# Group norms of a hybrid decoder layer: sums over partitions by two products of ones with the split squares, the sums issued a tick earlier, a small state tile in another pool, and the first masking of a state renewal placed later

## The chip, the cores and the metric

The kernel runs on one core of a Trainium2 chip. The time is that of one execution in device microseconds; the number for a kernel is the median of several executions. The times shown for the kernel before are 1761.23 us in the median of three, from 1761.22 to 1761.29.

## The reference, cut to what matters

One layer of a hybrid decoder runs over 320 tokens: 256 of a prompt and 64 (8 sequences of 8) that continue older sequences. A combined projection feeds a gated MLP and a state space mixer; their outputs go through one output projection, and a feed forward part with a short convolution follows. All of it is in 32-bit floats. The two places that the change touches are the norm inside the mixer, over four groups of 512 channels, and the recurrent states of the 8 continued sequences, which are renewed from their new tokens:

```python
y = y.reshape(bsz, L, SSM_WIDTH) * jax.nn.silu(z.astype(f32))
yg = y.reshape(bsz, L, SSM_GROUPS, SSM_WIDTH // SSM_GROUPS)
yg = yg * lax.rsqrt(jnp.mean(yg * yg, axis=-1, keepdims=True) + EPS)
y = yg.reshape(bsz, L, SSM_WIDTH) * norm_w.astype(f32)
...
up, new_conv = causal_depthwise_conv(up, conv_state, conv_w, conv_b)   # conv_ffn
```

## The kernel before, in words

**Layout and products.** Channels lie on the 128 partitions and the 320 tokens (`NT`) along the free axis. Every weight matrix comes in slabs of 512 KB (`slab`, DMA issued on SP at L126). ScalarE rounds a slab to the reduced format that TensorE streams in one pass (`whi`, L130), VectorE makes the rest (`wlo`, L132), each of `wraw`, `whi` and `wlo` in three buffers. Each 128x128 block then takes three matmuls of 320 columns (L143 to L145): high by high, high by low, low by high. A slab is 8 blocks, that is 24 matmuls.

**Order.** The program is written in the order of the products. Everything else hangs in a list of tasks (`bg`), Python generators of which `tick()` advances the first by one `yield` after a slab (after some slabs twice or three times, `rate`). A planner then sets each engine's own order from priorities and estimated times; `first()` raises a priority, and `tc.issue_after(x)` keeps an instruction behind `x`. Each engine runs its instructions strictly in its own order.

**Group norm** (`heads_out`, `norm`). For each of the four groups, `z_evac` builds `ssq` (128x320): per partition and token the sum of four squares. `norm` then needs the sum over the 128 partitions. `token_sums` (L284) takes three matmuls in full 32-bit floats, with 128 tokens of `ssq` as the stationary operand and one column of ones, which leave the sums as columns `tsum` with tokens on partitions. `rsqrt_of` (L250 to L256) takes the inverse root of these 128x3 numbers by eleven small VectorE instructions, a first guess and three Newton steps. `spread` (L292) brings the three columns back by three transposes, as a 128x320 tile in PSUM with the same value in every partition. VectorE multiplies the four tiles of `y` by it (L960; the tile is called `xs` in the profile), and `split` makes `ohi` and `olo` of them for the output projection (L373, L374; for the last group the buffers of `h_hi` and `h_lo` are used). `later` is the pair of ticks that `norm` lets pass before its sums and before `spread`.

**Convolution states of the feed forward part** (`ffn_up`). `fst` is a small tile (two buffers) of earlier rows; SP loads it at L1073. It lies in the pool `fp`, which takes the memory of pools that are closed before it.

**Renewal of states** (`renewals`). For each of four groups `tokens` loads decayed rows into `raw` by 16 small DMAs (L1180, tile `xb`). ScalarE copies them to `part` (L1191, `xb_parts`), VectorE masks the copy in place (L1194), and after some ticks TensorE takes four products of it (L1211, `up_ps`), which VectorE adds to the states `st` (L1213). GpSimd has multiplied the states by their decays before (L1199).

Of the kernel before, what the change touches and what calls it, by code (L numbers as in the profile page):

```python
# [9 lines left out]
F32 = mybir.dt.float32  # L10
F32R = mybir.dt.float32r
I32 = mybir.dt.int32
AF = mybir.ActivationFunctionType
ALU = mybir.AluOpType
# [3 lines left out]
P = 128  # L18
NP = 256
NB, TS = 8, 8  # L20
NS = NB * TS
NT = NP + NS
# [12 lines left out]
def hybrid_step(  # L35
# [14 lines left out]
    cp = ctx.enter_context(tc.tile_pool(name="cp", bufs=1))  # L50
# [6 lines left out]
    def misc(name):  # L57
        return ms.tile([P, 512], F32, tag="ms", name=name)
# [6 lines left out]
    with tc.high_priority(offset=300000):  # L65
        dve.memset(ones, 1.0)

        ps = misc("early")
        for _ in range(EARLY):
            pe.matmul(ps[:, :P], ones, ones, start=True, stop=True)  # L70
    upper = cp.tile([P, P], F32, name="upper")
    later = cp.tile([P, P], F32, name="later")
    bd2 = cp.tile([P, P], F32, name="bd2")
# [3 lines left out]
    bd = bd2[:NS, :NS]  # L77

    def masks():
        make_upper_triangular(nc, upper, 1.0, diag=True)  # L80
        make_lower_triangular(nc, later, 1.0, diag=False)
        pool.memset(bd2, 0.0)
        for op, fill, base in ((ALU.is_gt, 1.0, 1 - TS), (ALU.is_ge, 0.0, 0)):
            pool.affine_select(out=bd2, in_=bd2, pattern=[[-TS, P // TS], [0, TS]], compare_op=op, fill=fill, base=base,
                               channel_multiplier=1)

        d4 = ident.rearrange("p (i r t) -> p i r t", r=4, t=TS)
        dve.tensor_reduce(out=low[:, 0:1], in_=d4[:, :, 2:4], axis=mybir.AxisListType.XYZ, op=ALU.add)
        d5 = ident.rearrange("p (i k t) -> p i k t", k=2, t=TS)
        dve.tensor_reduce(out=low[:, 1:2], in_=d5[:, :, 1], axis=mybir.AxisListType.XY, op=ALU.add)  # L90
        dve.tensor_scalar(out=low, in0=low, scalar1=-1.0, scalar2=None, op0=ALU.mult)
        for r in range(2):
            rs = slice(64 * r, 64 * r + 64)
            dve.tensor_tensor(out=upper_s[rs], in0=upper[rs, rs], in1=bd2[rs, rs], op=ALU.mult)
        pool.memset(cmask, 1.0)
        cm4 = cmask.rearrange("p (h b) i -> p h b i", h=2)
        pool.affine_select(out=cm4, in_=cm4, pattern=[[0, 2], [-8, 4], [1, 32]],
                           compare_op=ALU.is_ge, fill=0.0, base=0, channel_multiplier=0)
        pool.affine_select(out=cm4, in_=cm4, pattern=[[0, 2], [8, 4], [-1, 32]],
                           compare_op=ALU.is_ge, fill=0.0, base=7, channel_multiplier=0)  # L100
# [8 lines left out]
    def first():  # L109

        return tc.high_priority(offset=200000)
# [130 lines left out]
        pd_last.append(made)  # L242


    def rsqrt_of(ss, scale, n, rows=P):

        v = tp.tile([P, n], F32, tag=f"rs_v{n}", name="rs_v")[:rows]
        r = tp.tile([P, n], F32, tag=f"rs_r{n}", name="rs_r", bufs=3)[:rows]
        t = tp.tile([P, n], F32, tag=f"rs_t{n}", name="rs_t")[:rows]
        dve.tensor_scalar(out=v, in0=ss, scalar1=scale, scalar2=EPS, op0=ALU.mult, op1=ALU.add)  # L250
        dve.tensor_scalar(out=r.bitcast(I32), in0=v.bitcast(I32), scalar1=-0.5, scalar2=float(0x5F3759DF),
                          op0=ALU.mult, op1=ALU.add)
        for _ in range(3):
            dve.scalar_tensor_tensor(out=t, in0=v, scalar=-0.5, in1=r, op0=ALU.mult, op1=ALU.mult)
            dve.tensor_tensor(out=t, in0=t, in1=r, op=ALU.mult)
            ins = dve.scalar_tensor_tensor(out=r, in0=t, scalar=1.5, in1=r, op0=ALU.add, op1=ALU.mult).ins  # L256
        rsqrt_ins.append(ins)
        return r
# [20 lines left out]
    def token_sums(sq, ps=None, more=False):  # L279

        begins = ps is None
        ps = misc("tsum") if begins else ps
        for c, o in enumerate((0, P, NT - P)):
            ins = pe.matmul(ps[:, c:c + 1], sq[:, o:o + P], ones[:, 0:1], start=begins and c == 0, stop=not more and c == 2).ins  # L284
        sums_ins.append(ins)
        return ps if more else ps[:, 0:3]

    def spread(r, out=None):

        ps = misc("spread")  # L290
        for c, o in ((2, NT - P), (0, 0), (1, P)):
            spread_ins.append(pe.transpose(ps[:, o:o + P], r[:, c:c + 1].to_broadcast([P, P]), ident).ins)  # L292
        if out is not None:
            act.copy(out, ps[:, :NT])
        return ps[:, :NT]
# [94 lines left out]
    with ExitStack() as mctx:  # L390
# [350 lines left out]
        with tc.tile_pool(name="sd", bufs=1) as sd:  # L741
# [192 lines left out]
            def heads_out(g, rate, later):  # L934

                ssq = hp.tile([P, NT], F32, tag="ssq", name="ssq")
                y = x_of.pop(g)

                def z_evac(j, ps):
                    if j == 0:  # L940
                        finish(tasks[g])
                    zs = tp.tile([P, NT], F32, tag="ev", name="zs", bufs=2)
                    with first():
                        scaled(ps, AF.Silu, zs)
                        dve.tensor_tensor(out=y[:, j, :], in0=y[:, j, :], in1=zs, op=ALU.mult)
                        add_square(ssq, y[:, j, :], j == 0, dve)
                project(w_in, Z0 + 512 * g, z_evac, quiet=4, rate=rate)

                def norm():
                    yield from repeat(None, later[0])  # L950
                    with tc.issue_after(newest[0]):
                        sums = token_sums(ssq)
                    with first():
                        r = rsqrt_of(sums, 1.0 / 512, 3)
                    yield from repeat(None, later[1])
                    rb = spread(r)

                    res[g] += [h[:, KD - 4:] for h in hT] if g == 3 else out_parts(hp, "o")
                    for j in range(4):
                        dve.tensor_tensor(out=y[:, j, :], in0=y[:, j, :], in1=rb, op=ALU.mult)  # L960
                        split(res[g][0][:, j, :], res[g][1][:, j, :], y[:, j, :], col(prm_at["norm"][3] + 4 * g + j))
                task = norm()
                bg.insert(0, task)
                return task
# [98 lines left out]
    with tc.tile_pool(name="fp", bufs=1) as fp:  # L1063
# [3 lines left out]
        ptf = fp.tile([P, 2 * NF, 2], F32, name="ptf")  # L1067

        def ffn_up(g):
            fst = fp.tile([P, 2, 4, NB, 2], F32, tag="fst", name="fst", bufs=2)  # L1070
            for half in range(2):
                k = NF * half + 4 * g
                sp.dma_start(fst[:, half], fconv[:, k:k + 4])  # L1073
# [81 lines left out]
        def renewals():  # L1155
# [18 lines left out]
            def tokens(g):  # L1174

                rows = xb_d[g].rearrange("(h i t) c -> i t h c", h=2, i=4)
                for i in range(4):
                    for r in range(4):
                        at = 32 * i + TS * r
                        sp.dma_start(raw[at:at + TS], rows[i])  # L1180
# [6 lines left out]
                tokens(0)  # L1187
            for g in range(4):
                h0 = 8 * g
                yield from repeat(None, 3)  # L1190
                act.copy(part, raw)  # L1191
                yield
                for at, m in ((slice(0, 512), 0), (slice(512, 640), 1)):
                    dve.scalar_tensor_tensor(out=part[:, :, at], in0=part[:, :, at].bitcast(F32), scalar=low[:, m:m + 1], in1=raw[:, :, at],  # L1194
                                             op0=ALU.mult, op1=ALU.add)
                for h in range(2):
                    st = ahead.pop(0)
                    for i in range(4):
                        pool.tensor_tensor(out=by_head(st[i]), in0=by_head(st[i]),  # L1199
                                           in1=tote[:, h0:h0 + 8, 4 * h + i:4 * h + i + 1].to_broadcast([P, 8, 64]), op=ALU.mult)  # L1200
                        yield
                    if h == 0:
                        ahead.append(load(g, 1))
                    elif g < 3:
                        ahead.append(load(g + 1, 0))
                        tokens(g + 1)
                    yield from repeat(None, 2)
                    grown = [misc("up_ps") for _ in range(4)]
                    for i in range(4):
                        at = slice(32 * i, 32 * i + 32)  # L1210
                        pe.matmul(grown[i], part[at, h, 512:], part[at, h, :512], start=True, stop=True, tile_position=(32 * i, 0))  # L1211
                    for i in range(4):
                        dve.tensor_tensor(out=st[i], in0=st[i], in1=grown[i], op=ALU.add)  # L1213
                        yield
                        act.dma_start(o_ssm_s[4 * h + i, g], st[i])
# [179 lines left out]
```

## Time and profile before

| | |
|---|---|
| median of three runs | 1761.23 us |
| the profiled execution's own time | 1762.04 us |
| its span in the trace | 1760.3 us |
| granted clock of TensorE | 0.999 |
| busy: TensorE, its weight loads | 1751.6 us, 1729.8 us |
| busy: VectorE, ScalarE, GpSimd | 1154.1 us, 806.6 us, 272.7 us |
| DMA | 301.38 MB, 171 GB/s in the mean |

TensorE is busy all through, so its own instructions are nearly the whole time. An idle stretch of another engine costs nothing by itself. The rows of the timeline below give the start of an instruction in us from the span's start, its length, engine, line and tiles. Matmuls overlap, so what one takes on TensorE is read from the distance between starts. A matmul in full 32-bit floats shows as two instructions, so three of them are "x6".

### The profile page before, as it was taken

Reading aid. Unit: us, or ns where it says so; the run is one execution under the profiler, and the core shown is the slowest. Engines: PE = TensorE matmul, PEld = TensorE weight load, DVE = VectorE, ACT = ScalarE, POOL = GpSimd, SP = SyncE. Lnnn points to the kernel's source line nnn. Section 1 sums busy time; section 2 is a strip of 40 time slices with the busy share of each in tenths; the row PEclk is TensorE's granted clock in tenths of the full one; section 3 lists DMA queues with packets and bytes.
Section 4 is the critical chain, followed back from the end, with each engine's and each line's share of the span. In section 5 each row is a group of like instructions: output and inputs, shape, how many; then the busy total and the mean of one; then the engine's idle time right before and its main releaser. Section 6 shows DMA issues by size and latency. Waiting matters only on the chain.

```text
span 1760.3 us, 31124 instructions
## 1 busy us (share of the span) xinstructions
PE 1751.6 (100%) x12178; PEld 1729.8 (98%) x12178; DVE 1154.1 (66%) x1949; ACT 806.6 (46%) x1172; POOL 272.7 (15%) x588
## 2 busy tenths in 40 slices
PE   9999999999999999999999999999999999999998
PEld 9999999999999999999999999999999999999997
DVE  7449754656767576668966677676657565656575
ACT  7344545333854445545544434343434343333335
POOL 1003200000111101021331212130201010111004
PEclk9999999999999999999999999999999999999999
DMA  7466655456665644554756666756454545454542
GB/s 248 144 167 182 185 151 150 153 155 190 216 206 163 201 145 131 166 161 143 228 169 223 189 217 195 222 185 192 151 153 148 156 148 155 148 155 147 155 151 104
DMA packets 228179, 301.38 MB, mean 171 GB/s; under 512 B 19936, under 2 KB 150848, under 8 KB 227840
## 3 DMA queue, kind: packets, MB, share of 16 engines
q1 hardware_dynamic: 215856, 281.27, 52.4%
q10 hardware_dynamic: 10640, 13.60, 2.2%
q0 software_dynamic: 1536, 4.52, 1.0%
q8 instruction: 96, 1.57, 0.4%
q14 instruction: 51, 0.42, 0.1%
HBM read 283.47 MB, written 15.61 MB: 170 GB/s over the span
## 4 chain that ended last, share of the span: by engine, by line
PE 95%; DVE 2%; DMA 1%; ACT 0%; POOL 0%; issue 0%; SPq 0%; POOLq 0%; DVEq 0%; ACTq 0%
PE ps L143 20%; PE ps L145 20%; PE ps L144 20%; PE pd L143 10%; PE pd L144 10%; PE pd L145 10%; PE y_ps L900 1%; DMA wraw<-in_ffn_w_up 1%; DVE wlo L132 1%; PE yo_ps L848 0%; PE sg L705 0%; PE tsum L284 0%; DVE h_lo L374 0%; DVE acc_mix L1042 0%; DMA vt<-in_xT 0%; ACT whi L130 0%
## 5 line engine op out<-in xcount | busy, mean ns | idle before, releaser
L132 DVE TENSOR_TENSOR wlo<-wraw,whi 128x1024 fp32r<-128x1024 f32 x470 | 582.9, 1241 | 436.9 <-ACT whi L130 434.9
L130 ACT CAST whi<-wraw 128x1024 fp32r<-128x1024 f32 x470 | 492.0, 1047 | 730.3 <-PE ps L144 437.7
L143 PE MATMUL ps<-h_hi,whi 128*128 128x320 f32 x2528 | 782.1, 310 | 0.4 <-ACT whi L130 0.4
L144 PE MATMUL ps<-h_lo,whi 128*128 128x320 f32 x2528 | 779.8, 309 | 0.0
L145 PE MATMUL ps<-h_hi,wlo 128*128 128x320 f32 x2528 | 777.8, 309 | 0.0
L143 PEld LDWEIGHTS ps<-h_hi,whi 128*128 128x128 f32 x2528 | 474.8, 188 | 4.2 <-issue 2.3
L144 PEld LDWEIGHTS ps<-h_lo,whi 128*128 128x128 f32 x2528 | 475.1, 188 | 0.0
L145 PEld LDWEIGHTS ps<-h_hi,wlo 128*128 128x128 f32 x2528 | 474.4, 188 | 0.1
L143 PE MATMUL pd<-fhi,whi 128*128 128x320 f32 x704 | 217.2, 309 | 0.0
L144 PE MATMUL pd<-flo,whi 128*128 128x320 f32 x704 | 217.0, 308 | 0.0
L145 PE MATMUL pd<-fhi,wlo 128*128 128x320 f32 x704 | 216.9, 308 | 0.0
L143 PE MATMUL pd<-ohi,whi 128*128 128x320 f32 x448 | 139.5, 312 | 0.0
L145 PE MATMUL pd<-ohi,wlo 128*128 128x320 f32 x448 | 138.5, 309 | 0.0
L144 PE MATMUL pd<-olo,whi 128*128 128x320 f32 x448 | 138.5, 309 | 0.0
L143 PEld LDWEIGHTS pd<-fhi,whi 128*128 128x128 f32 x704 | 132.2, 188 | 0.7 <-issue 0.7
L144 PEld LDWEIGHTS pd<-flo,whi 128*128 128x128 f32 x704 | 132.2, 188 | 0.2 <-issue 0.2
L145 PEld LDWEIGHTS pd<-fhi,wlo 128*128 128x128 f32 x704 | 132.2, 188 | 0.0
L1099 POOL COPY ptf<-pad 128x2 f32<-128x2 f32 x88 | 24.2, 275 | 508.3 <-DVE pad L1087 507.5
L236 DVE TENSOR_TENSOR acc_ffn<-acc_ffn,pd 128x320 f32<-128x320 f32 x160 | 77.2, 482 | 34.5 <-PE pd L145 33.6
L143 PEld LDWEIGHTS pd<-ohi,whi 128*128 128x128 f32 x448 | 84.0, 188 | 1.4 <-issue 0.7
L144 PEld LDWEIGHTS pd<-olo,whi 128*128 128x128 f32 x448 | 84.1, 188 | 0.2 <-issue 0.2
L145 PEld LDWEIGHTS pd<-ohi,wlo 128*128 128x128 f32 x448 | 84.1, 188 | 0.0
(301 smaller groups left out, 1513.6 us busy)
## 6 DMA issues: line engine op xcount, KB each, us to landing
wraw<-in_ffn_w_up SPq DMA_DIRECT2D x176, 512.0 KB
wraw<-in_w_in SPq DMA_DIRECT2D x142, 512.0 KB
wraw<-in_ffn_w_down SPq DMA_DIRECT2D x88, 512.0 KB
wraw<-in_w_out SPq DMA_DIRECT2D x64, 512.0 KB
st<-in_state_ssm SPq DMA_DIRECT2D x64, 256.0 KB
out_ssm_state_sample<-st ACTq DMA_DIRECT2D x32, 256.0 KB
cs<-dacs_d SPq DMA_DIRECT2D x16, 320.0 KB
xr<-in_xT SPq DMA_DIRECT2D x4, 640.0 KB
```

The lines of the kernel that those rows point to most:

```text
L130: act.copy(hi[:, :m], raw[:, :m])
L132: dve.tensor_tensor(out=lo[:, :m], in0=raw[:, :m], in1=hi[:, :m].bitcast(F32), op=ALU.subtract)
L143: pe.matmul(ps, whi, xhi, start=first, stop=False)
L144: pe.matmul(ps, whi, xlo, start=False, stop=False)
L145: newest[0] = pe.matmul(ps, wlo, xhi, start=False, stop=last).ins
L236: dve.tensor_tensor(out=acc[:, nb, :], in0=acc[:, nb, :], in1=ps[:, :NT], op=ALU.add)
L900: pe.matmul(ps[64 * i:64 * i + 64, cols], w(hl), x(hl, m, cpx), tile_position=(0, 64 * i), **flags)
L1099: pool.tensor_copy(ptf[:, k, :], pad[:, 256:258])
```

## The change

The sum over partitions of a group norm is formed by two matmuls of 320 columns whose stationary operand is a 128x128 matrix of ones (`ones_r`, made once at the start) and whose streamed operands are the two parts of `ssq`, which ScalarE and VectorE make one tick before. The result stands in every partition, so `spread` is left out there, and `rsqrt_of` works on 128x320 elements in place of 128x3, into a tile `rb` in SBUF. In the task the split stands two ticks before the place of the old sums, and the sums one tick before it; the scaling of `y` keeps its tick. `token_sums` and `spread` stay in use elsewhere. `fst` moves from the pool `fp` to the pool `cp`, which is open from the start. In `renewals` the first group's copy and masking stand after the four multiplications of its first half and eight more ticks; the other groups keep their order, with one more pause.

```diff
--- before.py
+++ after.py
@@ -68,6 +68,7 @@
         ps = misc("early")
         for _ in range(EARLY):
             pe.matmul(ps[:, :P], ones, ones, start=True, stop=True)
+    ones_r = cp.tile([P, P], F32R, name="ones_r")
     upper = cp.tile([P, P], F32, name="upper")
     later = cp.tile([P, P], F32, name="later")
     bd2 = cp.tile([P, P], F32, name="bd2")
@@ -77,6 +78,7 @@
     bd = bd2[:NS, :NS]
 
     def masks():
+        dve.tensor_copy(ones_r, ones)
         make_upper_triangular(nc, upper, 1.0, diag=True)
         make_lower_triangular(nc, later, 1.0, diag=False)
         pool.memset(bd2, 0.0)
@@ -242,11 +244,10 @@
         pd_last.append(made)
 
 
-    def rsqrt_of(ss, scale, n, rows=P):
-
-        v = tp.tile([P, n], F32, tag=f"rs_v{n}", name="rs_v")[:rows]
-        r = tp.tile([P, n], F32, tag=f"rs_r{n}", name="rs_r", bufs=3)[:rows]
-        t = tp.tile([P, n], F32, tag=f"rs_t{n}", name="rs_t")[:rows]
+    def rsqrt_of(ss, scale, n, rows=P, places=None):
+
+        v, r, t = places or (tp.tile([P, n], F32, tag=f"rs_{name}{n}", name=f"rs_{name}", bufs=bufs)[:rows]
+                             for name, bufs in (("v", 2), ("r", 3), ("t", 2)))
         dve.tensor_scalar(out=v, in0=ss, scalar1=scale, scalar2=EPS, op0=ALU.mult, op1=ALU.add)
         dve.tensor_scalar(out=r.bitcast(I32), in0=v.bitcast(I32), scalar1=-0.5, scalar2=float(0x5F3759DF),
                           op0=ALU.mult, op1=ALU.add)
@@ -947,13 +948,20 @@
                 project(w_in, Z0 + 512 * g, z_evac, quiet=4, rate=rate)
 
                 def norm():
-                    yield from repeat(None, later[0])
+                    yield from repeat(None, later[0] - 2)
+                    parts = [tp.tile([P, NT], F32R, tag="pv", name="ssq_part", bufs=4) for i in range(2)]
+                    with first():
+                        split(*parts, ssq)
+                    yield
+                    ps = misc("tsum")
                     with tc.issue_after(newest[0]):
-                        sums = token_sums(ssq)
+                        for i in range(2):
+                            pe.matmul(ps[:, :NT], ones_r, parts[i], start=i == 0, stop=i == 1)
                     with first():
-                        r = rsqrt_of(sums, 1.0 / 512, 3)
-                    yield from repeat(None, later[1])
-                    rb = spread(r)
+                        rb = sd.tile([P, NT], F32, tag="rb", name="rb", bufs=1)
+                        v, t = (tp.tile([P, NT], F32, tag="pv", name=f"rs_{n}", bufs=4) for n in "vt")
+                        rsqrt_of(ps[:, :NT], 1.0 / 512, NT, places=(v, rb, t))
+                    yield from repeat(None, later[1] + 1)
 
                     res[g] += [h[:, KD - 4:] for h in hT] if g == 3 else out_parts(hp, "o")
                     for j in range(4):
@@ -1067,7 +1075,7 @@
         ptf = fp.tile([P, 2 * NF, 2], F32, name="ptf")
 
         def ffn_up(g):
-            fst = fp.tile([P, 2, 4, NB, 2], F32, tag="fst", name="fst", bufs=2)
+            fst = cp.tile([P, 2, 4, NB, 2], F32, tag="fst", name="fst", bufs=2)
             for half in range(2):
                 k = NF * half + 4 * g
                 sp.dma_start(fst[:, half], fconv[:, k:k + 4])
@@ -1187,12 +1195,17 @@
                 tokens(0)
             for g in range(4):
                 h0 = 8 * g
-                yield from repeat(None, 3)
-                act.copy(part, raw)
-                yield
-                for at, m in ((slice(0, 512), 0), (slice(512, 640), 1)):
-                    dve.scalar_tensor_tensor(out=part[:, :, at], in0=part[:, :, at].bitcast(F32), scalar=low[:, m:m + 1], in1=raw[:, :, at],
-                                             op0=ALU.mult, op1=ALU.add)
+                yield from repeat(None, 4)
+
+                def parts():
+
+                    act.copy(part, raw)
+                    yield
+                    for at, m in ((slice(0, 512), 0), (slice(512, 640), 1)):
+                        dve.scalar_tensor_tensor(out=part[:, :, at], in0=part[:, :, at].bitcast(F32), scalar=low[:, m:m + 1], in1=raw[:, :, at],
+                                                 op0=ALU.mult, op1=ALU.add)
+                if g:
+                    yield from parts()
                 for h in range(2):
                     st = ahead.pop(0)
                     for i in range(4):
@@ -1204,6 +1217,9 @@
                     elif g < 3:
                         ahead.append(load(g + 1, 0))
                         tokens(g + 1)
+                    if g == 0 and h == 0:
+                        yield from repeat(None, 8)
+                        yield from parts()
                     yield from repeat(None, 2)
                     grown = [misc("up_ps") for _ in range(4)]
                     for i in range(4):
```

The planner's order changes with it. VectorE around the sums of the first group (`rs_v`, `rs_r` or `rb`, and `rs_t` are the steps of the inverse root; `wlo` belongs to the weight slabs), before:

```order
L302 TENSOR_TENSOR ssq<-ssq,sq 128x320
L132 TENSOR_TENSOR wlo<-wraw,whi 128x1024 x3
L250 TENSOR_SCALAR rs_v<-tsum 128x3
L251 TENSOR_SCALAR rs_r<-rs_v 128x3
L254 SCALAR_TENSOR_TENSOR rs_t<-rs_v,rs_r 128x3
L255 TENSOR_TENSOR rs_t<-rs_t,rs_r 128x3
L256 SCALAR_TENSOR_TENSOR rs_r<-rs_t,rs_r 128x3
L132 TENSOR_TENSOR wlo<-wraw,whi 128x1024
```

The same engine and place now:

```order
L303 TENSOR_TENSOR ssq<-ssq,sq 128x320
L134 TENSOR_TENSOR wlo<-wraw,whi 128x1024
L372 TENSOR_TENSOR ssq_part<-ssq,ssq_part 128x320
L134 TENSOR_TENSOR wlo<-wraw,whi 128x1024
L251 TENSOR_SCALAR rs_v<-tsum 128x320
L252 TENSOR_SCALAR rb<-rs_v 128x320
L134 TENSOR_TENSOR wlo<-wraw,whi 128x1024
L255 SCALAR_TENSOR_TENSOR rs_t<-rs_v,rb 128x320
L256 TENSOR_TENSOR rs_t<-rs_t,rb 128x320
L257 SCALAR_TENSOR_TENSOR rb<-rs_t,rb 128x320
```

The low part of `ssq` is made behind the first slab, and the inverse root begins behind the second slab in place of the third.

TensorE at the first products of the renewed states (`pd` are blocks of the down projection, `ps` of the next up projection), before:

```order
L145 MATMUL pd_10_10400<-fhi,wlo 128x320
L143 MATMUL pd_10_10400<-fhi,whi 128x320
L1211 MATMUL up_ps<-xb_parts 128x512 x4
L144 MATMUL pd_10_10400<-flo,whi 128x320
L145 MATMUL pd_10_10400<-fhi,wlo 128x320
```

And now:

```order
L147 MATMUL ps_3_10487<-h_hi,wlo 128x320
L145 MATMUL ps_3_10487<-h_hi,whi 128x320
L146 MATMUL ps_3_10487<-h_lo,whi 128x320
L147 MATMUL ps_3_10487<-h_hi,wlo 128x320
L1227 MATMUL up_ps<-xb_parts 128x512 x4
L145 MATMUL ps_0_10484<-h_hi,whi 128x320
```

The four products stand 137 matmuls of weights later, behind the end of a slab in the next up projection. In ScalarE's and VectorE's orders the first copy and masking stand behind as many slabs as before (250).

SP around the load of `fst`, before:

```order
L126 DMA wraw<-in_ffn_w_up 128x4x256 x2
L1073 DMA fst<-in_fconv 128x64 x3
L126 DMA wraw<-in_ffn_w_up 128x4x256
L1073 DMA fst<-in_fconv 128x64
L126 DMA wraw<-in_ffn_w_up 128x4x256
```

Now these four loads stand behind the 16th slab of the input projection:

```order
L449 DMA dt_w<-in_w_in 128x16x32
L128 DMA wraw<-in_w_in 128x2x512
L1081 DMA fst<-in_fconv 128x64 x4
L128 DMA wraw<-in_w_in 128x2x512
L128 DMA wraw<-in_w_in 128x4x256 x2
```

They moved ahead by some 200 slabs, and the slabs of the up projection follow each other on SP without them.

## The prediction

> **What bounds the kernel now.** I read the page's busy times and its chain first, then who waited for whom on TensorE, then the timeline at the places that the diff names.
>
> ```profile
> PE 1751.6 (100%) x12178; PEld 1729.8 (98%) x12178; DVE 1154.1 (66%) x1949; ACT 806.6 (46%) x1172; POOL 272.7 (15%) x588
> ...
> PE 95%; DVE 2%; DMA 1%; ACT 0%; POOL 0%; issue 0%; SPq 0%; POOLq 0%; DVEq 0%; ACTq 0%
> ```
>
> TensorE is busy for 1751.6 of 1760.3 us, and 95% of the chain runs through it. So the time changes by what TensorE is given or spared, and by its few waits. These are the longest:
>
> ```profile
> PE tsum L284 <- DVE sq L302: 0.7, 1, 0.7
> PE up_ps L1211 <- DVE xb_parts L1194: 0.6, 1, 0.6
> ```
>
> The change touches both: `up_ps` directly, the other (a sum ahead of the up projection) by way of the loads of `fst`.
>
> **The price of a slot.** On a steady stretch:
>
> ```profile
> 533.78 0.31 PE L144 MATMUL ps<-h_lo,whi 128*128 128x320 f32 x1
> ...
> 536.57 0.31 PE L145 MATMUL ps<-h_hi,wlo 128*128 128x320 f32 x1
> 536.72 0.72 PE L284 MATMUL tsum<-ones,ssq 128*128 128x1 f32 x6
> 537.30 0.39 PE L143 MATMUL ps<-h_hi,whi 128*128 128x320 f32 x1
> 537.53 0.31 PE L144 MATMUL ps<-h_lo,whi 128*128 128x320 f32 x1
> ...
> 544.28 0.31 PE L145 MATMUL ps<-h_hi,wlo 128*128 128x320 f32 x1
> 544.42 0.49 PE L292 MATMUL spread<-ident,rs_r 128*128 128x128 f32 x3
> 544.67 0.40 PE L143 MATMUL ps<-h_hi,whi 128*128 128x320 f32 x1
> 544.90 0.31 PE L144 MATMUL ps<-h_lo,whi 128*128 128x320 f32 x1
> ```
>
> The first two rows are 19 matmuls apart: 2.79 / 19 = 0.147 us for one of 320 columns.
>
> **Part 1, the sums.** Between 536.57 and 537.53 two ordinary matmuls would have taken 0.294 us; it took 0.96, so the sums cost 0.666 us. The same way the spread costs 0.62 - 0.294 = 0.326 us. The second group shows the same distances, 0.96 and 0.62, and I take them for the third; in the last the spread also waited:
>
> ```profile
> 634.01 0.31 PE L145 MATMUL ps<-h_hi,wlo 128*128 128x320 f32 x1
> ...
> 634.97 0.31 PE L144 MATMUL ps<-h_lo,whi 128*128 128x320 f32 x1
> ...
> 641.72 0.31 PE L145 MATMUL ps<-h_hi,wlo 128*128 128x320 f32 x1
> ...
> 642.34 0.31 PE L144 MATMUL ps<-h_lo,whi 128*128 128x320 f32 x1
> ...
> 755.32 0.31 PE L144 MATMUL pd<-olo,whi 128*128 128x320 f32 x1
> 755.64 0.51 PE L292 MATMUL spread<-ident,rs_r 128*128 128x128 f32 x3
> 755.91 0.40 PE L145 MATMUL pd<-ohi,wlo 128*128 128x320 f32 x1
> 756.14 0.30 PE L143 MATMUL pd<-ohi,whi 128*128 128x320 f32 x1
> ```
>
> In the last it is 0.82 - 0.294 = 0.526 us. Removed: 4 x 0.666 + 3 x 0.326 + 0.526 = 4.17 us. Added: eight matmuls in the form of the weight products (320 columns, reduced format), so 8 x 0.147 = 1.18 us. Net -2.99 us. The trace has no product with a matrix of ones in that format. From below its bound is 0.147 us, which the streamed columns set in every weight product; from above it is one such matmul behind a change of kind, 0.23 us (544.67 to 544.90), which would take back 8 x 0.083 = 0.66 us. I take 0.147, since form and format are those of the neighbours.
>
> A rule of the Trainium skill speaks against this: "TensorE: Matmul & The Clock Gate", section "Back-to-back issue gap", gives a matmul of 1 to 64 columns about 60 cycles, and 134 for 128 columns. By it six one-column passes and three transposes would cost about 0.32 us (an estimate from that page), and the change would spare next to nothing. The rows, 0.666 and 0.326 us, decide.
>
> **What the sums wait for now.** They need both parts of `ssq`. In the first two groups they stand more than a slab behind it. The last two are tighter; the fourth:
>
> ```profile
> 747.27 0.49 DVE L302 TENSOR_TENSOR ssq<-ssq,sq 128x320 f32<-128x320 f32 x1
> 747.68 0.48 DVE L236 TENSOR_TENSOR acc_mix<-acc_mix,pd 128x320 f32<-128x320 f32 x1
> 748.21 1.23 DVE L132 TENSOR_TENSOR wlo<-wraw,whi 128x1024 fp32r<-128x1024 f32 x1
> ```
>
> By the new order the low part follows this `wlo`, so it ends near 749.4 + 0.5 = 749.9. The old sums began here at 750.54, at the same place in TensorE's order: some 0.65 us spare, and no wait.
>
> **VectorE.** Per group eleven steps on 128x3 become eleven on 128x320, and one subtraction comes in. ScalarE gets one copy.
>
> ```profile
> L960 DVE TENSOR_TENSOR xs<-xs,spread 128x320 f32<-128x320 f32 x16 | 7.4, 482 | 4.2 <-PE spread L292 4.2
> L374 DVE SCALAR_TENSOR_TENSOR olo<-xs,prm,ohi 128x320 fp32r<-128x320 f32 x12 | 6.2, 545 | 0.0
> L254 DVE SCALAR_TENSOR_TENSOR rs_t<-rs_v,rs_r 128x3 f32<-128x3 f32 x12 | 1.9, 161 | 0.3
> ```
>
> With the kernel's own widths: 6 x 0.545 + 6 x 0.482 - 11 x 0.161 = +4.4 us a group, 17.6 in all. The cover, by stages (busy time of PE, PEld, DVE, ACT, POOL):
>
> ```profile
> 526.00:546.00 20.00, 20.00 (x141) 19.99 (x140) 9.29 (x20) 7.08 (x9) 0.00 (x0) 1.00 0.52 156
> 546.00:571.00 25.00, 25.00 (x215) 24.58 (x214) 23.80 (x46) 14.16 (x26) 5.18 (x19) 1.00 0.57 176
> 747.00:767.00 20.00, 19.99 (x140) 19.75 (x139) 16.37 (x38) 8.54 (x11) 0.00 (x0) 1.00 0.46 150
> ```
>
> In the first group the wide steps fall into 526 to 546, where VectorE idles 10.7 us, and the crowded stage behind gets shorter, because the scaling, which waited for `spread`, comes sooner. In the last group 3.6 us are free for 4.4; the rest delays a `wlo` by about 1 us. `rs_v` waits for the sums with a `wlo` queued behind it, but a slab's two parts are made early:
>
> ```profile
> 536.77 1.05 ACT L130 CAST whi<-wraw 128x1024 fp32r<-128x1024 f32 x1 [2.43 <-PE ps L144]
> ```
>
> `whi` begins when TensorE has read the slab three back (its third buffer), two slabs of 24 x 0.147 us or 7.0 us ahead, and 1.05 + 1.23 us of work leave 4.7. No more than six wide steps (3.1 us) stand between two slabs. Cost on the path: 0. `ones_r`, one VectorE step in the first idle microseconds, costs 0.
>
> **Two waits that go.** `ohi` was late at the start of two output projections:
>
> ```profile
> PEld pd L143 <- ACT ohi L373: 0.3, 2, 0.2
> ```
>
> The new order makes `ohi` a slab sooner: -0.3 us. Against it, the transposes of the fourth group's `xs` are cut into five runs, before into four, and a turn back to weight products costs 0.23 - 0.147 = 0.08 us. They also stand 34 matmuls (5 us) earlier, behind convolutions that the new order of VectorE brings forward too; how far, no row shows, and I allow a wait of 0 to 4 slots, 0.6 us.
>
> **Part 2, the first renewal.**
>
> ```profile
> 939.82 0.31 PE L143 MATMUL pd<-fhi,whi 128*128 128x320 f32 x1
> 940.71 0.50 PE L1211 MATMUL up_ps<-xb_parts 32*128 32x512 f32 x4 [0.59 <-DVE xb_parts L1194]
> ```
>
> 0.89 - 0.147 = 0.74 us are lost. Now the four products stand 137 matmuls (20 us) later and the masking behind the same slab: no wait, -0.74 us. Nothing else waits at it, since `st` is added five slabs behind as before.
>
> **Part 3, `fst`.** SP stood for 4.6 us before it could load `fst`, with a slab queued behind:
>
> ```profile
> SPq L1073 <- DVE acc_mix L1044: 4.6, 1, 4.6
> 831.10 1.65 SPq L1073 DMA_DIRECT2D fst<-in_fconv  x3
> 832.86 0.38 SPq L126 DMA_DIRECT2D wraw<-in_ffn_w_up  x1
> 837.13 1.05 ACT L130 CAST whi<-wraw 128x1024 fp32r<-128x1024 f32 x1 [4.49 <-DMA wraw<-in_ffn_w_up]
> 830.88 1.22 DVE L132 TENSOR_TENSOR wlo<-wraw,whi 128x1024 fp32r<-128x1024 f32 x1
> ```
>
> The slab lands at 837.1 and ScalarE waits for it. But its buffer comes free only with the `wlo` that ends at 832.1, so without `fst` it is issued 0.75 us sooner, not 4.6. The next slab depends on the next `wlo` and gains nothing directly. The chain from there to the 0.7 us wait at the sum shortens by something between 0 and the whole stall of 0.86 us. I take 0.3, which the possible wait of 0 to 0.6 at the transposes cancels at its middle. At the new place the four loads stand in front of one slab, at 0.4 us each of SP's time, where no TensorE wait is shown: 0.
>
> **Sum.** -2.99 - 0.74 - 0.30 + 0.08 = -3.95 us. The span goes from 1760.3 to 1756.35, the profiled time from 1762.04 to 1758.1, and the median, 0.81 below that, from 1761.23 to 1757.3. A difference of 0.2%, 3.5 us, is about the least that a measurement of this kernel tells from none; the forecast lies just beyond it. Own range: -3.95 - 0.86 = -4.8 to -3.95 + 0.9 = -3.05 (the transposes at 0.6, some of the dearer products), so 1756.4 to 1758.2. Chance 0.60.
>
> **Rivals.** *The new sums wait for the split.* ScalarE and VectorE must each serve a slab before the parts in groups three and four, with 0.65 us spare. If one slips behind another slab step, the sums come 1.05 + 1.23 - 0.65 = 1.6 us late, twice 3.2 us, and 0.8 remain of the gain: 1760.5. For it: the thin margin; against it: `first()` on the split, and the order above. With half slips between it and the forecast, 0.23.
>
> *VectorE becomes the bound (slower).* The 17.6 us of wide steps stand in front of slabs. They decide once more than 4.0 us reach TensorE, which needs the 4.7 us of lead to be used up in several groups. All of them exposed gives 1757.3 + 17.6 = 1774.9. For it: 23.8 of 25 us busy in the stage behind; against it: 10.7 us idle just where the steps fall. 0.07.
>
> *The rule of short passes.* If the short instructions mostly filled gaps that TensorE would have had anyway, what goes is worth no more than the 1.18 us that come, and the two waits of 0.74 and 0.30 remain: 1760.2. The distances in the rows speak against it: 0.03. The page named above is its ground.
>
> *More goes than I count*, other small waits with it: under 1756.4, to about 1755: 0.07.
>
> **How the numbers follow.** 1755.8 to 1759.8 takes in the forecast's range, most of the better case and half of the first rival. Faster by over 0.2% (under 1757.7) takes some 0.5 of the forecast's 0.60 and the better case: 0.57. Slower by over 0.2%: VectorE as bound, 0.07. Within 0.2%: 0.36.
>
> **What would show it.** No `spread` but the five outside the group norms; `tsum` with `ones_r` at 0.29 us a pair; no wait of `up_ps` for `xb_parts` and of `pd` for `ohi`; the wait at the sum ahead of the up projection at 0 to 0.7 us. A wait of `tsum` for `ssq_part` proves the first rival, waits of TensorE for `wlo` the second, and a gain under 3 us without either means that the pair costs more than two slots.

## The result, and the profile after

The changed kernel takes 1757.56 us in the median of 21 runs, against 1761.22 us for the kernel before beside it: a ratio of 0.9981, with a 95% interval of 0.9975 to 0.9987, or -3.66 us. One run, with a granted clock of 0.851, is not in the ratio. Forecast were 1757.3 us and a range of 1755.8 to 1759.8. The profiled execution took 1757.2 us with a span of 1755.3 us, 4.84 us less than the profiled one of before; two single executions differ here by more than the medians do, since that of before lies 0.82 us above its kernel's median and that of after 0.36 below.

The busy times of the page, and from the waits the groups of TensorE:

```profile
PE 1747.5 (100%) x12150; PEld 1725.9 (98%) x12150; DVE 1170.4 (67%) x1954; ACT 808.2 (46%) x1176; POOL 278.7 (16%) x588
...
PE ps L145 <- ACT whi L132: 0.8, 2, 0.4
PE tsum L285 <- DVE sq L303: 0.4, 1, 0.4
```

TensorE has 4.1 us less of its own work, VectorE 16.3 us more (forecast: 17.6). The waits of `up_ps` for `xb_parts` and of `pd` for `ohi` are gone, and nothing on TensorE waits for `ssq_part`. TensorE's timeline at the sums of the first and the fourth group, then VectorE's at the fourth:

```profile
532.86 0.31 PE L147 MATMUL ps<-h_hi,wlo 128*128 128x320 f32 x1
533.01 0.45 PE L959 MATMUL tsum<-ssq_part,ones_r 128*128 128x320 f32 x2
...
533.44 0.31 PE L146 MATMUL ps<-h_lo,whi 128*128 128x320 f32 x1
...
747.93 0.46 PE L959 MATMUL tsum<-ssq_part,ones_r 128*128 128x320 f32 x2
748.23 0.31 PE L145 MATMUL pd<-ohi,whi 128*128 128x320 f32 x1
...
746.74 0.48 DVE L372 TENSOR_TENSOR ssq_part<-ssq,ssq_part 128x320 fp32r<-128x320 f32 x1
```

From the last weight product ahead (532.86) to the second one behind (533.44) is 0.58 us, less two slots 0.29: the pair takes two slots (a slot is the 0.147 us of one weight product), without the 0.083 us of a change of kind. In the fourth group the low part ends at 747.22, 0.71 us before the products (forecast: 0.65).

The whole trace can be cut at five instructions that both kernels have: the first norm's sum, the sum ahead of the output's norm, the sum and the spread ahead of the up projection, and the last sum. Of before, then of after:

```profile
31.24 0.83 PE L284 MATMUL tsum<-ones,acc_mix 128*128 128x1 f32 x6 [0.34 <-DVE acc_mix L601]
801.49 0.80 PE L284 MATMUL tsum<-ones,sq 128*128 128x1 f32 x6
850.01 0.80 PE L284 MATMUL tsum<-ones,sq 128*128 128x1 f32 x6 [0.70 <-DVE sq L302]
853.25 0.49 PE L292 MATMUL spread<-ident,rs_r 128*128 128x128 f32 x3
1743.76 0.83 PE L284 MATMUL tsum<-ones,sq 128*128 128x1 f32 x6
```

```profile
31.05 0.83 PE L285 MATMUL tsum<-ones,acc_mix 128*128 128x1 f32 x6 [0.30 <-DVE acc_mix L602]
797.98 0.80 PE L285 MATMUL tsum<-ones,sq 128*128 128x1 f32 x6
845.41 0.31 PE L145 MATMUL ps_one<-h_hi,whi 128*128 128x320 f32 x1
846.14 0.80 PE L285 MATMUL tsum<-ones,sq 128*128 128x1 f32 x6 [0.42 <-DVE sq L303]
849.38 0.49 PE L293 MATMUL spread<-ident,rs_r 128*128 128x128 f32 x3
1739.26 0.83 PE L285 MATMUL tsum<-ones,sq 128*128 128x1 f32 x6
```

The group norms' part (first to second row) went from 770.25 to 766.93 us, -3.32. The part of the renewals (the last two rows) went from 890.51 to 889.88, -0.63. The stall at the sum ahead of the up projection (from `ps_one` at 845.41 to `tsum` at 846.14, less a slot) is 0.58 us after 0.86. The rest of the 5.0 us by which the spans differ is 0.19 at the start, 0.08 ahead of the stall and 0.51 behind TensorE's last instruction.

### The profile page after: what moved, and what is told of

It is laid out like the page before. It is cut to its first block, busy times and chain, and to the rows that moved or that the text cites. A ratio compares the mean times of both kernels' runs of the same rounds, so it can differ in the third digit from the quotient of the medians.

```text
span 1755.3 us, 31062 instructions
## 1 busy us (share of the span) xinstructions
PE 1747.5 (100%) x12150; PEld 1725.9 (98%) x12150; DVE 1170.4 (67%) x1954; ACT 808.2 (46%) x1176; POOL 278.7 (16%) x588
## 4 chain that ended last, share of the span: by engine, by line
PE 96%; DVE 2%; DMA 1%; ACT 0%; POOL 0%; issue 0%; SPq 0%; POOLq 0%; DVEq 0%; ACTq 0%
PE ps L145 20%; PE ps L147 20%; PE ps L146 20%; PE pd L145 10%; PE pd L146 10%; PE pd L147 10%; PE y_ps L901 1%; DVE wlo L134 1%; DMA wraw<-in_ffn_w_up 0%; PE yo_ps L849 0%; PE sg L706 0%; DVE h_lo L375 0%; DVE acc_mix L1050 0%; DMA vt<-in_xT 0%; PE vt_ps L591 0%; DVE acc_mix L1052 0%
## 5 line engine op out<-in xcount | busy, mean ns | idle before, releaser
L1107 POOL COPY ptf<-pad 128x2 f32<-128x2 f32 x88 | 28.7, 326 | 472.0 <-DVE pad L1095 471.2
```

The source lines that it names most:

```text
L1107: pool.tensor_copy(ptf[:, k, :], pad[:, 256:258])
```

## The experiments

All were timed beside the kernel before (medians 1761.2 to 1761.5 us). The table gives for each its median and, from the trace of its one profiled execution, the same cuts in us.

| kernel | median | 31 to 798 | stall at the sum | sum to spread | spread to last sum |
|---|---|---|---|---|---|
| before | 1761.22 | 770.25 | 0.86 | 3.24 | 890.51 |
| after | 1757.56 | 766.93 | 0.58 | 3.24 | 889.88 |
| e1, norms' part alone | 1758.56 | 766.94 | 1.41 | 3.24 | 890.63 |
| e2, renewal alone | 1760.72 | 770.24 | 0.76 | 3.25 | 890.31 |
| e3, `fst` alone | 1761.38 | 770.27 | 0.18 | 3.24 | 890.51 |
| e4, before, short passes twice | 1764.76 | 773.99 | 0.00 | 3.19 | 890.50 |
| e5, after, root twice | 1769.15 | 777.80 | 1.36 | 3.24 | 889.88 |
| e7, after, pair twice | 1760.88 | 768.09 | 1.74 | 4.80 | 889.87 |
| e9, after, `fst` back | 1757.70 | 766.93 | 1.23 | 3.24 | 889.89 |
| e10, after, last square first | 1757.00 | 766.93 | 0.00 | 3.22 | 889.87 |
| e12, after, sums at the old place | 1758.61 | 767.61 | 1.53 | 4.79 | 889.86 |
| e13, after, one Newton step less | 1758.28 | 767.46 | 1.39 | 4.68 | 889.97 |

**The three parts alone (e1, e2, e3).** Each is the kernel before with the lines of one part of the diff above.

> The kernel before with the group norms' part alone. Forecast, by its own terms: -4.17 + 1.18 - 0.30 + 0.08 = -3.2 us against before. If the sums waited for the split (first rival): about 0 to -0.8. If VectorE became the bound: slower by several us. In the profile: no wait of the products of ones, 0.29 us a pair.

> The kernel before with the later first masking alone. Forecast: -0.74 us, the whole stall ahead of the first four products of the renewal. If another wait took its place: 0. A wait of TensorE for the masked copy at the new place would show it.

> The kernel before with the small state tile in the other pool alone. Forecast: the stall of 0.86 us at the sum ahead of the up projection shrinks by about 0.3 us (bounds 0 and 0.86), so -0.3 us or not measurable. If the 4.6 us that SP waited were on the path: -0.9 us, the whole stall gone.

The ratios are 0.9984 (0.9975 to 0.9992), 0.9996 (0.9987 to 1.0005) and 0.9999 (0.9990 to 1.0007); by the medians -2.92, -0.76 and -0.10 us, together -3.78. The first is the change; the intervals of the other two take in no change at all. In e1 the norms' part of the trace shrank by 3.31 us, close to the forecast's 3.2, but the stall behind it grew to 1.41 us. In e2 the wait is gone from TensorE's groups; another of 0.37 us at 1066.57, which no other trace has, hides most of it in the one trace.

**What the short passes cost (e4).** On the kernel before:

```diff
-                        sums = token_sums(ssq)
+                        sums = token_sums(ssq, token_sums(ssq, more=True))
...
-                        r = rsqrt_of(sums, 1.0 / 512, 3)
+                        r = rsqrt_of(sums, 0.5 / 512, 3)
...
-                    rb = spread(r)
+                    rb = spread(r, times=2)
```

> The kernel before with the six one-column passes and the three transposes of each group norm issued twice (the root takes half the scale for the sums, the second transposes write the same values again). If their price is the distance in the rows: six more passes cost 6 x 0.11 = 0.67 us and three more transposes up to 0.33 us a group, 3 to 4 us in all. If they mostly filled gaps that TensorE would have had anyway: under 1.2 us. The Trainium skill, "TensorE: Matmul & The Clock Gate", section "Back-to-back issue gap", would by its cycles make it about 1.3 us (an estimate).

Ratio 1.0018 (1.0010 to 1.0027), +3.28 us. TensorE at the sums and at the spread of the first group:

```profile
536.35 0.31 PE L145 MATMUL ps<-h_hi,wlo 128*128 128x320 f32 x1
536.49 1.39 PE L284 MATMUL tsum<-ones,ssq 128*128 128x1 f32 x12
...
537.98 0.31 PE L144 MATMUL ps<-h_lo,whi 128*128 128x320 f32 x1
...
544.73 0.31 PE L145 MATMUL ps<-h_hi,wlo 128*128 128x320 f32 x1
544.87 0.82 PE L292 MATMUL spread<-ident,rs_r 128*128 128x128 f32 x6
...
545.68 0.31 PE L144 MATMUL ps<-h_lo,whi 128*128 128x320 f32 x1
```

From 536.35 to 537.98, less two slots, is 1.34 us: the second set of six passes cost 0.67 us, just what the first does. From 544.73 to 545.68 it is 0.66 us in the same way, so the second three transposes cost 0.33 us, again as much as the first. The part to 798 grew by 3.74 us; the stall behind, which shrank to nothing, gave 0.86 back. So the rule of short passes from the prediction is out: the passes are not hidden in gaps, and the expectation's estimate of 1.3 us is far too low.

**What the new pair costs (e7).** On the changed kernel:

```diff
-                        for i in range(2):
-                            pe.matmul(ps[:, :NT], ones_r, parts[i], start=i == 0, stop=i == 1)
+                        for i in range(4):
+                            pe.matmul(ps[:, :NT], ones_r, parts[i % 2], start=i == 0, stop=i == 3)
...
-                        rsqrt_of(ps[:, :NT], 1.0 / 512, NT, places=(v, rb, t))
+                        rsqrt_of(ps[:, :NT], 0.5 / 512, NT, places=(v, rb, t))
```

> The changed kernel with the two products of ones of each group norm issued twice (half the scale in the root), so eight more matmuls. Forecast: 8 x 0.147 = +1.18 us. If each cost a change of kind, 8 x 0.23 = +1.84 us. If the weight loads of the matrix of ones did not overlap: more than 2 us.

The median, 1760.88, is 3.3 us above the changed kernel's; taken alone it would speak for the third case, weight loads that don't overlap. But the eleven runs lie in two heaps: five from 1758.74 to 1759.45, six from 1760.88 to 1761.74. The part to 798 grew by 1.16 us, which is the forecast's 1.18 and the lower heap. The traced execution, 1760.96 us, is one of the upper heap, and its trace shows where the rest went: to the sum ahead of the up projection. The windows behind show the granted clock in the third column from the right:

```profile
846.39 0.31 PE L145 MATMUL ps_one<-h_hi,whi 128*128 128x320 f32 x1
848.28 1.05 PE L285 MATMUL tsum<-ones,sq 128*128 128x1 f32 x6 [1.58 <-DVE sq L303]
...
849.61 0.47 PE L147 MATMUL ps_one<-h_hi,wlo 128*128 128x320 f32 x1
849.88 0.47 PE L145 MATMUL ps_one<-h_hi,whi 128*128 128x320 f32 x1
...
848.00:850.00 2.00, 1.72 (x9) 1.75 (x10) 0.72 (x4) 0.21 (x1) 0.00 (x0) 0.67 0.44 95
850.00:852.00 2.00, 2.00 (x9) 2.00 (x8) 1.93 (x6) 0.00 (x0) 0.00 (x0) 0.50 0.47 173
852.00:854.00 2.00, 2.00 (x16) 1.99 (x15) 0.54 (x1) 0.39 (x1) 0.00 (x0) 0.98 0.92 273
```

Behind a stall of 1.74 us the granted clock is halved for 3.4 us, from 848.68 to 852.09: a slot takes 0.27 us (849.61 to 849.88), and the way from the sum to the spread 4.80 us in place of 3.24. One stall so costs 1.6 us beyond itself. That the other five runs of the heap lost their time in the same way is likely, but no trace of them shows it.

**VectorE's room (e5, e13).** The inverse root run twice, and the root without its third Newton step:

```diff
-                        rsqrt_of(ps[:, :NT], 1.0 / 512, NT, places=(v, rb, t))
+                        for _ in range(2):
+                            rsqrt_of(ps[:, :NT], 1.0 / 512, NT, places=(v, rb, t))
```

```diff
-        for _ in range(3):
+        for _ in range(2 if places else 3):
```

> The changed kernel with the wide inverse root of each group norm run twice (the second run writes the same values), so 11 more wide steps a group, about 5.2 us, 21 us on VectorE in all. Forecast (VectorE's wide steps lie beside TensorE's work): by the changed kernel's timeline the last low part of the scaled tiles is ready 4.9 us before its use or more in groups one to three, and some 1.7 us in the fourth, so +3 to +4 us, nearly all in the fourth group. If VectorE were already the bound there (second rival): +15 to +21 us. If it had room everywhere: 0.

> The changed kernel without the third Newton step of the four wide inverse roots (left out of the computation), three wide steps or 1.5 us a group, 6 us less on VectorE. If the wide steps lie wholly beside TensorE's work, as forecast: 0. If part of them is on the path: faster, by up to 6 us.

Twice costs 11.6 us more than the changed kernel takes (ratio to before 1.0044, 1.0032 to 1.0057). TensorE's waits, and the place of the longest:

```profile
PE pd L145 <- ACT h_hi L374: 3.7, 1, 3.7
PE pd L145 <- ACT ohi L374: 1.5, 1, 1.5
PE tsum L285 <- DVE sq L303: 1.2, 1, 1.2
...
PE pd L146 <- DVE olo L375: 0.7, 1, 0.7
...
773.41 0.31 PE L147 MATMUL pd<-ohi,wlo 128*128 128x320 f32 x1
777.41 0.56 PE L145 MATMUL pd<-h_hi,whi 128*128 128x320 f32 x2 [3.69 <-ACT h_hi L374]
```

My expectation was too low. Measured at weight products that both traces have, the fourth group loses 6.8 us, since the clock falls to half behind the wait of 3.7, and the first two, which I had taken as covered, lose 1.4 and 2.7 us as well. So about half of a second dose of wide steps reaches TensorE. That any of the first dose does is not seen: 6 us less on VectorE (e13) made the kernel no faster, 1758.28 (ratio 0.9986, 0.9977 to 0.9994). Its trace is longer than that of after by 0.53 us in the part to 798, of which 0.31 are a wait at one transposition in VectorE's and ScalarE's new order, and by a stall of 1.39 us with the halved clock behind it.

**The sums back at the old place (e12).** In the changed kernel the sums of the first two groups stand one slab sooner than before (533.0 in place of 536.7 us in the first). Here they stand where they did:

```diff
-                    yield from repeat(None, later[0] - 2)
+                    yield from repeat(None, later[0] - 1)
...
-                    yield from repeat(None, later[1] + 1)
+                    yield from repeat(None, later[1])
```

> The changed kernel with the split and the products of ones one tick later, so that the products stand at the place of the old sums; the scaling keeps its place. If the sooner place only brings the two waits for ohi (forecast: 0.30 us): +0.3 us. If VectorE has no room to run the wide root in one tick less (5.4 us of steps): scaled tiles late in two or more groups, +2 us and more.

1758.61 us (ratio 0.9986, 0.9977 to 0.9995). The part to 798 is 0.68 us longer than after, between the two expectations. Of it 0.32 us are the two waits for `ohi`, as forecast; another 0.34 us is a wait at 667 us for a tile of GpSimd's (`xde`), which the expectation did not have. No other scaled tile came late, so VectorE had the room. The rest of its trace's excess is a stall of 1.53 us with the halved clock.

**Does `fst` matter more in the changed kernel? (e9)**

```diff
-            fst = cp.tile([P, 2, 4, NB, 2], F32, tag="fst", name="fst", bufs=2)
+            fst = fp.tile([P, 2, 4, NB, 2], F32, tag="fst", name="fst", bufs=2)
```

> The changed kernel with the small state tile back in its old pool, nothing else. If the tile's move is worth what it is on the kernel before (0.1 us by the medians): +0.1 us. If it matters more once TensorE arrives sooner at the sum ahead of the up projection (the stall there was 1.41 us with the norms' part alone, 0.58 with all parts, 0.86 before): about +0.8 us.

1757.70 us, 0.14 above (ratio 0.9980, 0.9971 to 0.9988). No.

**The stall itself (e10).** In the changed kernel's trace the last addition of squares stands behind a low part of 1.2 us, on VectorE:

```profile
841.58 2.87 DVE L303 TENSOR_TENSOR sq<-sq,sq 128x320 f32<-128x320 f32 x5
844.37 1.22 DVE L134 TENSOR_TENSOR wlo<-wraw,whi 128x1024 fp32r<-128x1024 f32 x1
845.51 0.49 DVE L303 TENSOR_TENSOR sq<-sq,sq 128x320 f32<-128x320 f32 x1
```

```diff
+            with tc.issue_after(behind) if behind else nullcontext():
-            dve.tensor_tensor(out=lo[:, :m], in0=raw[:, :m], in1=hi[:, :m].bitcast(F32), op=ALU.subtract)
+                dve.tensor_tensor(out=lo[:, :m], in0=raw[:, :m], in1=hi[:, :m].bitcast(F32), op=ALU.subtract)
...
-                    wb = slab(rows_of(ffn_w_up, 8 * i, 8, DFF + 256, P))
+                    wb = slab(rows_of(ffn_w_up, 8 * i, 8, DFF + 256, P), squared[0] if i else None)
```

Here `squared[0]` is the last addition of squares, and the two instructions change places; nothing else moves in VectorE's or TensorE's order.

> The changed kernel with one swap on VectorE: the last addition of squares ahead of the up projection's sum stands before a slab's low part in place of behind it (1.2 us). If the stall there (0.58 us in the changed kernel's trace, 1.23 to 1.74 us in those of three experiments) is set by that order: the stall under 0.2 us in the trace, the median -0.4 us against the changed kernel's 1757.6, and hardly any run at 1759.5 or more, where the halved clock behind a longer stall (the trace with the pairs issued twice) would have put them. If the stall is set by the slab's arrival alone: no difference.

1757.0 us, the fastest of all (ratio 0.9976, 0.9965 to 0.9986), with all eight runs between 1756.21 and 1757.86. VectorE, then TensorE:

```profile
841.89 3.47 DVE L304 TENSOR_TENSOR sq<-sq,sq 128x320 f32<-128x320 f32 x6
...
845.38 0.31 PE L146 MATMUL ps_one<-h_hi,whi 128*128 128x320 f32 x1
845.53 0.78 PE L286 MATMUL tsum<-ones,sq 128*128 128x1 f32 x6
```

The stall is gone, and not because the slab came early: the `whi` on which it hangs (next section) began 38.40 us behind the sum at 798, which in the old order would make a stall of 0.9 us. Against the changed kernel the intervals overlap, so that the 0.56 us is shown by the trace and not by the times alone.

**The first norm in the same way (e8, e11).** The products of ones in place of `token_sums` and `spread` at 31 us; e11 has one `yield` more than e8:

```diff
-                    sums = token_sums(acc[:, 0, :])
+                    split(*parts, acc[:, 0, :])
...
+                        pe.matmul(ps[:, :NT], ones_r, parts[i], start=i == 0, stop=i == 1)
...
+                    rsqrt_by_root(ps[:, :NT], 1.0 / D, places=(v, w, r1, s))
```

> The changed kernel with the first norm, at 31 us, formed in the same way: its sum of squares is split, two products of ones, the inverse root on 128x320, no spread. Forecast: there the sums cost 1.24 us with their wait (30.44 to 31.97, less two slots) and the spread 0.33, the pair 0.29, so up to -1.28 us against the changed kernel. Rival: the wide root, about 3 us in place of 0.9, makes the first evacuations late and TensorE waits for a free accumulator: 0 or slower.

> The first norm by the two products of ones again, now with one more pause, so that the columns of dt keep their place in the order (with one pause less TensorE waited 2.7 us for them). Forecast: up to -1.28 us against the changed kernel, less a wait of 0.4 us for the split, so about -0.9 us: 1756.7. Rival: the wide root makes the first evacuations late, and TensorE waits for an accumulator: 0 or slower.

Slower both: 1763.14 and 1762.70 us. VectorE in e11, and TensorE's longest wait:

```profile
34.11 2.15 DVE L268 RECIPROCAL rs_w<-rs_v 128x320 f32<-128x320 f32 x1
...
39.81 1.67 DVE L363 TENSOR_TENSOR ev<-ps,r 128x320 f32<-128x320 f32 x4
...
PE dt_four L456 <- POOL dt_w L450: 3.2, 1, 3.2
```

The wide reciprocal alone takes 2.15 us, and the first evacuations come at 39.8 in place of 35.0. The planner set the products of `dt`, which stand at 53.8 us in the changed kernel, into the hole, and there they wait for their operand; behind that wait, too, the clock is halved (granted clock 0.50 from 40.00 to 43.35). The same edit so loses 5 us here. How much of that is the late root alone, and how much the planner's new place for `dt`, no run separates.

## Why the prediction was right

**Part 1.** The forecast for the norms' part was -2.99 - 0.30 + 0.08 = -3.21 us; the trace has -3.32, the same in after, e1, e9 and e10 to 0.01. Compared at the weight products that before and after share, the terms hold one by one, so the sum is no luck: the first group loses 0.67 us of sums and 0.33 of spread and gets 0.29 for its pair, the last spread gives 0.53, the two waits for `ohi` give 0.16 each, and the transposes take 0.04 (forecast: 0.08). The prices held singly too: 0.67 us for six passes and 0.33 for three transposes (e4), 0.145 us for a product of ones (e7: 1.16 us for eight). The bound of 0.23 us for such a product is out.

**VectorE.** Path cost 0 held (no wait behind the wide steps in after's trace, and e13), but the margin is smaller than the argument from idle time made it: the window of the fourth group is busy 19.16 of 20 us now, and another dose of steps costs half its length (e5).

```profile
745.00:765.00 20.00, 20.00 (x139) 20.00 (x138) 19.16 (x36) 7.66 (x10) 0.00 (x0) 1.00 0.46 151
```

**Part 2.** -0.74 was forecast; the trace shows -0.63. The term missed that the turn from weight products to the four is paid at the new place too, as at every renewal:

```profile
956.05 0.31 PE L147 MATMUL ps<-h_hi,wlo 128*128 128x320 f32 x1
956.29 0.51 PE L1227 MATMUL up_ps<-xb_parts 32*128 32x512 f32 x4
```

0.24 us less a slot is 0.09 us, and so much of the 0.74 was no wait.

**Part 3** was taken at -0.3 and cancelled against a wait at the transposes. Both are nearly nothing: 0.10 and 0.14 us by the medians (e3, e9), and 0.04 at the transposes. The argument on the issue held: without `fst` in front, the slab goes out 0.75 us sooner (30.62 in place of 31.37 us behind the sum at 798), and the next one at the same 33.6 us. SP's 4.6 us were off the path.

**The step that failed** is the wait at the sum ahead of the up projection, which I let shrink from 0.86 to between 0 and 0.7 us. In the changed kernel's own trace it is 0.58, but 1.23 to 1.74 in all six of its relatives in the table that keep VectorE's order there (e1, e5, e7, e9, e12, e13). What sets it is the start of one `whi` some 38 us behind the sum at 798, which waits for its slab; the squares stand behind it on ScalarE and reach VectorE in one chain. ScalarE at that place in before, in e4 and in e12:

```profile
839.90 1.05 ACT L130 CAST whi<-wraw 128x1024 fp32r<-128x1024 f32 x1 [0.99 <-DMA wraw<-in_ffn_w_up]
```

```profile
842.50 1.05 ACT L130 CAST whi<-wraw 128x1024 fp32r<-128x1024 f32 x1 [0.88 <-DMA wraw<-in_ffn_w_up]
```

```profile
837.66 1.05 ACT L132 CAST whi<-wraw 128x1024 fp32r<-128x1024 f32 x1 [1.44 <-DMA wraw<-in_ffn_w_up]
```

That is 38.41, 37.50 and 39.01 us behind the sum (801.49, 805.00, 798.65), with stalls of 0.86, 0.00 and 1.53 us: each microsecond by which it comes later than 37.5 is one of stall. All the kernels of the table but e10 lie on that line within 0.06 us. It is not that TensorE arrives too soon, as my expectation of e9 had it: e5 reaches this stage 7 us later than before and stalls 1.36 us. Nor does the pool of `fst` decide it (e3 0.18, after 0.58, e5 1.36; before 0.86, e9 1.23). Nor is it SP: in every kernel of the table the slab is issued 33.5 to 33.7 us behind the sum. What differs is the time from there until ScalarE can begin, from 3.9 us (e4) to 5.4 (e12), during which SP issues two more slabs. (In e3 and e7 ScalarE waits for the slab ahead and comes to this one late.) Why it is mostly longer beside the new norms stays open; one trace of each kernel can't tell a rule from scatter.

The terms that repeat from trace to trace add up to -3.32 - 0.08 - 0.63 = -4.03 us. A saving that the forecast did not have comes on top: TensorE's last instruction ends 4.65 to 4.67 us ahead of the span's end in every trace with the new norms, 5.16 in before's (4.80 in e2's). Of these 0.51 us, 0.24 are lost again outside the span: a time exceeds its span by 1.95 us in the changed kernel's median, by 1.71 in before's. What causes either is open. That makes -4.3 us, and the medians show -3.66. The 0.6 us between them would fit stalls that grew where I let them shrink: before's 0.86 stands in an execution 0.82 us above its median, after's 0.58 in one 0.36 below, so the two traces don't show the stall of a median run. The forecast's -3.95 so comes close to the medians with some luck, a saving it lacked against a stall it had too small. Four of the 21 runs, at 1759.45 to 1760.23 us, lie 2 to 3 us above the others, as runs with the halved clock would: e10, whose stall is gone, has none, but in eight runs only. No trace of such a run of the changed kernel itself was taken.

**The rivals.** No wait for the split and none for `wlo` at the norms in the trace, so the first two are out; the rule of short passes fell with e4. "More goes than I count" put the time under 1756.4; neither the changed kernel's median nor e10's, 1757.0, is there.

## What to carry to other kernels

A sum over partitions by full 32-bit one-column passes and transposes is dear on a busy TensorE: 1.0 us here against 0.29 for two wide products that leave the result already spread, if another engine has 5 us of idle time for the wide arithmetic behind it; at the first norm, where little covers that, the same edit lost 5 us together with the order that came with it. A forecast for a whole kernel is only as good as its least steady stall: look for the next place where TensorE waits, and put the last step of the late operand ahead of work that has time (e10). Cut two traces at instructions that both have: parts that repeat to 0.01 us tell more than medians with 1 us of scatter.

## What was not expected of the hardware

A stall of 1.4 to 1.7 us can halve TensorE's granted clock for 3.4 us, at 1.4 to 1.6 us extra. It did behind 1.39, 1.53 and 1.74 us (e13, e12, e7) and did not behind 1.36 and 1.41 us (e5, e1), nor behind 1.48 us (e8) and 1.66 us (e5, at 648 us). In e13 the first five products behind the stall still ran at full speed:

```profile
846.98 0.80 PE L285 MATMUL tsum<-ones,sq 128*128 128x1 f32 x6 [1.24 <-DVE sq L303]
...
848.31 0.35 PE L147 MATMUL ps_one<-h_hi,wlo 128*128 128x320 f32 x1
848.46 0.47 PE L145 MATMUL ps_one<-h_hi,whi 128*128 128x320 f32 x1
848.73 0.47 PE L146 MATMUL ps_one<-h_lo,whi 128*128 128x320 f32 x1
```

So length alone doesn't decide it. The Trainium skill, "TensorE: Matmul & The Clock Gate", section "Part 1: The HAM clock gate (the "warmup" mystery)", has the clock set by activity in a free-running window of about 3.4 us, and half speed after an idle window. The time at half speed (3.4 us each time, in e7 from 848.68 to 852.09) and the dependence on more than the length agree with such a window; that a whole window must be idle does not, since stalls of about half that length were enough.
